# Layer 0's gathered context rows: 16 instead of 45 of the second tile's picks are left to the beginning of layer 1

## The chip, the cores and the metric

The kernel runs on one core of a Trainium2 chip. The metric is the device time of one execution in microseconds (us); lower is better. PE is TensorE, DVE is VectorE, ACT is ScalarE, POOL is GpSimd, SP is the SyncE queue that issues most transfers.

## What is computed

Two layers of a hybrid mixer (RWKV-7, latent attention and Hyena side by side) work on 512 latent and 256 context tokens of width 1024. Each layer ends in a PEER feed-forward: every token picks 16 of 16,384 one-neuron experts in each of 8 heads, so 128 picks a token:

```python
act = jax.nn.gelu(jnp.einsum('thkd,td->thk', exp_u[e_idx], xc), approximate=False)
return jnp.einsum('thk,thkd->td', gate * act, exp_v[e_idx])
```

In layer 0 the feed-forward serves both streams; the context's result is needed as input of layer 1's context projection.

## The kernel before

The program is written for a framework that orders the instructions of each engine by priority (mostly program order) and gives each engine one queue in that order. An engine works its queue off strictly in order.

**Layer 0's feed-forward (`ffn`, L1509)** treats its six 128-token tiles in two ways. Four latent tiles go through a *dense pass*: a loop over 128 blocks `n` of 128 experts. For a block the kernel loads `uT` (scores, 512 KB) and the second half of `uv` (values, 512 KB), rounds each into a high and a low part (`wh` by ACT at L657, `wl` by DVE at L658), multiplies the tokens by `uT` (`product`), applies gelu (`g`, ACT, L1544), multiplies by the gate weights `W` (DVE, L1608; a 1 MB load `W<-Wd` every four blocks), splits the result (`ch` ACT, `cl` DVE, L1612) and multiplies by the values. Three tiles accumulate in PSUM, the fourth (`acc3`) is added up by DVE at L1635, two blocks at a time, out of the PSUM tag `mm`, which has two buffers and serves the scores too. The scores of 44 of the 128 blocks are made earlier (`early`) and only loaded (`gl<-gd`). The loads go into a ring of three buffers `w`: SP issues a load when DVE has finished the `wl` of three loads before.

**Gathered rows (`Picks`, L181).** The two context tiles go another way: for pick `k` of a tile, POOL issues one indirect transfer (L203) that brings, for each of 128 tokens, the 8 KB row of the chosen expert (1 MB in all). DVE multiplies its first half by the tokens and sums (L219), ACT does gelu and the gate (L236, L237), DVE adds the second half into `acc` (L241). There are 256 such picks: 128 of the first context tile, then 128 of the second. Five row buffers are used in the dense pass, four behind it.

**Who does how many.** `NP = picks.n - REST` (L1590) is the number that the dense pass fetches: it spreads them over its blocks in proportion to `done`, so many scored blocks of `total = 212`:

```python
base, NP = len(picks.rows), picks.n - (0 if li else REST)
...
picks.fetch(min(base + 3 + (NP - base) * done // total, NP))
```

The other `REST` picks of the second tile are fetched by `gather` from `context_out`, one of four program tracks that `weave` merges at layer 1's beginning by a virtual clock; each pick advances that clock by `GC = 2.8`:

```python
while len(p.rows) < p.n - rest:
    p.fetch(len(p.rows) + 1)
    yield cost
p.use(p.n - rest)
```

After the last pick `ffn_out` transposes `acc` (L1503), scales it and stores the context. Beside this track run: `project` (the latents' projection with 21 weight tiles of 512 KB, 8 fp32 matrix products each, `mm<-h,wh`; each tile advances the clock by 6), then the context's projection, which waits for the context and for the filters; `hyena_filters` (two halves with products `hy<-...`, DVE writes `st`, which is stored as `coef<-st`); and later the RWKV scan.

Of the kernel before, what the change touches and what calls it, by code (L numbers as in the profile page):

```python
# [151 lines left out]
PB, RL, ML = 0.7, 0.42, 1.0  # L152
HL, HL1 = 1.0, 1.0
GP = 0.0
REST, GC = 45, 2.8
GS = 2.0 ** 14
SK = 44
WB, GB, UD = (2, 2), (1, 1), 1
# [1646 lines left out]
```

## Time and profile before

| what | value |
|---|---|
| median of 3 runs | 5381.51 us (5369.8 to 5392.99) |
| the profiled execution's own time | 5380.15 us |
| its span, first to last instruction | 5378.2 us |
| PE busy | 4894.6 us (91%) |
| DVE busy | 3836.6 us (71%) |
| mean granted TensorE clock | 0.935 |
| transfers | 1028.17 MB, mean 191 GB/s |

The profile is of one execution; 1.95 us of its time lie outside its span. Layer 0's dense pass runs from about 1834 to 3019 us, the beginning of layer 1 that this change touches from there to about 3320 us. A busy share over the whole span says little about either; the rows below are cut to these stretches.

### The profile page before, as it was taken

The page shows a single profiled execution, that of the slowest core. Times are in us where ns is not written, and L with a number is a line of the kernel's source. Part 1 is how long each engine was busy: PE and PEld are TensorE (multiplying, and loading weights), DVE is VectorE, ACT ScalarE, POOL GpSimd, SP SyncE. Part 2 cuts the span into 40 slices and gives each one's busy share as a digit, 9 for nine tenths or more (in the row PEclk, how much of TensorE's full clock was granted, in tenths as well). Part 3 has the DMA queues.
Part 4 walks back from the last instruction along what each step waited for, and adds up shares of the span by engine and source line. Part 5 has one row for each costly group of instructions (what it writes and reads, how often), then busy time and mean ns, then how long its engine had stood idle before and what let it go on. Part 6 is the DMA issues. An engine that isn't in the chain of part 4 may idle for free. (4 is left out here: it accounts for less than half of the span.)

```text
span 5378.2 us, 75892 instructions
## 1 busy us (share of the span) xinstructions
PE 4894.6 (91%) x28685; PEld 3719.0 (69%) x28685; DVE 3836.6 (71%) x8311; ACT 1918.1 (36%) x3416; POOL 1118.1 (21%) x869
## 2 busy tenths in 40 slices
PE   7987898889989999999999789888889999999998
PEld 4765676546746788877877435656647578888887
DVE  6456766755898688878888874766646986777776
ACT  5322222343256433333333222222223354444442
POOL 2222211222200122222222241211122101111110
PEclk8987898889999999999999889877889999999999
DMA  6300121342266888888888873200022678888885
GB/s 199 111 26 30 53 87 56 98 142 91 95 180 206 272 315 323 318 317 311 319 315 315 300 282 125 73 1 1 1 75 81 199 223 302 320 323 311 327 316 207
DMA packets 392491, 1028.17 MB, mean 191 GB/s; under 512 B 31443, under 2 KB 198644, under 8 KB 336572
## 3 DMA queue, kind: packets, MB, share of 16 engines
q1 hardware_dynamic: 336828, 620.64, 34.4%
q0 software_dynamic: 55296, 402.68, 19.7%
q8 instruction: 225, 3.69, 0.3%
q14 instruction: 142, 1.16, 0.1%
HBM read 920.19 MB, written 103.02 MB: 190 GB/s over the span
## 5 line engine op out<-in xcount | busy, mean ns | idle before, releaser
L203 POOL DMA_INDIRECT row<-in_uv,idx x384 | 535.6, 1395 | 2033.7 <-DVE acc L241 1853.8
L657 ACT ACTIVATE wh<-w 128x1024 fp32r<-128x1024 f32 x535 | 566.6, 1060 | 1037.0 <-PE mm L272 471.1
L272 PE MATMUL mm<-hlo,wh 128*128 128x512 f32 (+2 forms) x2400 | 863.9, 364 | 16.4 <-DVE acc L1635 6.8
L272 PE MATMUL mm<-hhi,wh 128*128 128x512 f32 (+2 forms) x2400 | 859.9, 362 | 0.0
L658 DVE TENSOR_TENSOR wl<-w,wh 128x1024 fp32r<-128x1024 f32 x466 | 568.4, 1223 | 295.5 <-ACT wh L657 272.7
L272 PE MATMUL mm<-hhi,wl 128*128 128x512 f32 (+2 forms) x2400 | 523.6, 359 | 0.0
L272 PEld LDWEIGHTS mm<-hlo,wh 128*128 128x128 f32 x2400 | 456.0, 190 | 84.0 <-issue 9.9
L241 DVE SCALAR_TENSOR_TENSOR acc<-row,act,acc 128x1024 f32<-128x1024 f32 x381 | 491.8, 1291 | 30.4 <-ACT act L237 29.9
L272 PEld LDWEIGHTS mm<-hhi,wh 128*128 128x128 f32 x2400 | 456.6, 190 | 60.1 <-issue 4.5
L219 DVE SCALAR_TENSOR_TENSOR row<-row,xk 128x1024 f32<-128x1024 f32 x384 | 473.2, 1233 | 18.3 <-DMA row<-in_uv,idx 17.3
L272 PEld LDWEIGHTS mm<-hhi,wl 128*128 128x128 f32 x2400 | 421.9, 188 | 51.7 <-issue 1.9
L272 PE MATMUL mm<-row,wh 128*128 128x384 f32 (+1 forms) x736 | 296.6, 546 | 6.7 <-ACT g L1544 4.4
L236 ACT ACTIVATE act<-act 128x1 f32<-128x1 f32 x384 | 75.9, 198 | 527.8 <-DVE row L219 527.6
L658 POOL TENSOR_TENSOR wl<-w,wh 128x1024 fp32r<-128x1024 f32 x69 | 165.8, 2408 | 424.5 <-PE mm L272 226.0
L1781 ACT ACTIVATE stage<-ch 128x512 f32<-128x512 f32 x224 | 220.4, 1110 | 64.3 <-PE ch L272 63.5
L272 PEld LDWEIGHTS mm<-row,wh 128*128 128x128 f32 x736 | 134.0, 193 | 113.8 <-issue 67.2
L272 PE MATMUL rw<-wh,cl 128*128 128x512 f32 x512 | 202.0, 394 | 7.7 <-DMA w<-in_uT 3.2
L272 PE MATMUL mm<-h,wh 128*128 128x512 f32 (+1 forms) x480 | 193.7, 550 | 13.4 <-DMA w<-in_hw 10.6
L272 PE MATMUL rw<-wl,ch 128*128 128x512 f32 x512 | 201.3, 393 | 0.0
L272 PE MATMUL rw<-wh,ch 128*128 128x512 f32 x512 | 200.4, 391 | 0.0
L272 PE MATMUL ch<-wh,cl 128*128 128x512 f32 x512 | 200.4, 391 | 0.0
L272 PE MATMUL ch<-wh,ch 128*128 128x512 f32 x512 | 200.0, 391 | 0.0
(541 smaller groups left out, 10296.2 us busy)
## 6 DMA issues: line engine op xcount, KB each, us to landing
w<-in_uv SPq DMA_DIRECT2D x256, 512.0 KB
w<-in_uT SPq DMA_DIRECT2D x210, 512.0 KB
Wd<-stage SPq DMA_DIRECT2D x28, 2048.0 KB
w<-in_mod_w SPq DMA_DIRECT2D x192, 256.0 KB
W<-Wd SPq DMA_DIRECT2D x32, 1024.0 KB
W<-Wd SPq DMA_DIRECT2D x32, 768.0 KB
wh<-in_uT SPq DMA_DIRECT2D x46, 512.0 KB
w<-in_wq SPq DMA_DIRECT2D x32, 512.0 KB
```

The lines of the kernel that those rows point to most:

```text
L203: self.nc.gpsimd.indirect_dma_start(out=row, out_offset=None, in_=self.k.io[f"uv{self.li}"], in_offset=bass.IndirectOffsetOnAxis(ap=self.t ...
L219: nc.vector.scalar_tensor_tensor(row[:, 0:1024], row[:, 0:1024], 1.0, self.x, op0=OP.mult, op1=OP.mult, accum_out=act)
L236: nc.scalar.activation(act, act, AF.Gelu)
L241: nc.vector.scalar_tensor_tensor(self.acc, row[:, 1024:], act, self.acc, op0=OP.mult, op1=OP.add)
L272: self.nc.tensor.matmul(out, lhsT, rhs, start=start, stop=stop, skip_group_check=True)
L657: self.nc.scalar.activation(wh[:, s], w, AF.Copy)
L658: eng.tensor_tensor(wl[:, s], w, wh[:, s].bitcast(F32), op=OP.subtract)
L1781: nc.scalar.activation(stage[:, :, u:u + 4].rearrange("p a t -> p t a"), p, AF.Copy, scale=1 / GS)
```

## The change

One number. `GC` and the code stay as they are.

```diff
-REST, GC = 45, 2.8
+REST, GC = 16, 2.8
```

So `NP` becomes 240 instead of 211, and `gather` in `context_out` fetches 16 rows instead of 45. The framework's order moves accordingly. Three places are shown.

POOL's queue where layer 1 begins; the two MEMSETs prepare layer 1's context keys and values, L203 is a gathered row of the second context tile, L1296 and L1297 belong to the Hyena filters. Before:

```order
L203 DMA row<-in_uv,idx_11414 128x2048 x122
L203 DMA row<-in_uv,idx_11415 128x2048 x92
L460 MEMSET kTc 1x1536
L462 MEMSET Vc 128x6x64
L203 DMA row<-in_uv,idx_11415 128x2048 x16
L1296 TENSOR_TENSOR hs<-hh 128x256
L1297 TENSOR_TENSOR hd<-hh 128x256
L203 DMA row<-in_uv,idx_11415 128x2048
```

The same place in the changed kernel:

```order
L203 DMA row<-in_uv,idx_11414 128x2048 x121
L203 DMA row<-in_uv,idx_11415 128x2048 x120
L460 MEMSET kTc 1x1536
L462 MEMSET Vc 128x6x64
L203 DMA row<-in_uv,idx_11415 128x2048 x8
L1296 TENSOR_TENSOR hs<-hh 128x256
L1297 TENSOR_TENSOR hd<-hh 128x256
L1296 TENSOR_TENSOR hs<-hh 128x256
```

Behind the MEMSETs stood 36 gathers (16 in one piece, 20 strewn between filter work), and now stand 8; ahead of them there are 28 more.

DVE's queue in the dense pass, from the `cl` of its tenth block on (`row,act<-row,xk` and `acc<-row` are the two halves of a pick, `wl` the low part of a load, `acc_16907` the fourth tile's sum). Before:

```order
L1612 TENSOR_TENSOR cl<-g,ch 128x512
L219 SCALAR_TENSOR_TENSOR row,act<-row,xk 128x1024
L241 SCALAR_TENSOR_TENSOR acc<-row,act,acc 128x1024
L658 TENSOR_TENSOR wl<-w,wh 128x1024
L1635 TENSOR_TENSOR acc_16907<-acc_16907,mm 128x512 x2
L658 TENSOR_TENSOR wl<-w,wh 128x1024
L1612 TENSOR_TENSOR cl<-gl,ch 128x512
```

In the changed kernel:

```order
L1612 TENSOR_TENSOR cl<-g,ch 128x512
L219 SCALAR_TENSOR_TENSOR row,act<-row,xk 128x1024
L241 SCALAR_TENSOR_TENSOR acc<-row,act,acc 128x1024
L658 TENSOR_TENSOR wl<-w,wh 128x1024
L1635 TENSOR_TENSOR acc_16907<-acc_16907,mm 128x512
L219 SCALAR_TENSOR_TENSOR row,act<-row,xk 128x1024
L241 SCALAR_TENSOR_TENSOR acc<-row,act,acc 128x1024
L1635 TENSOR_TENSOR acc_16907<-acc_16907,mm 128x512
L658 TENSOR_TENSOR wl<-w,wh 128x1024
L1612 TENSOR_TENSOR cl<-gl,ch 128x512
```

A second pick has moved in between the two sums, ahead of the next `wl`. Over the whole dense pass DVE's queue holds 241 picks instead of 214.

DVE's queue at layer 1's beginning, where the first filter's coefficients `st` are written (L685 and L686 are the convolution of a projected tile). Before:

```order
L1322 TENSOR_TENSOR st<-hy,rhy 128x2x128
L219 SCALAR_TENSOR_TENSOR row,act<-row,xk 128x1024
L241 SCALAR_TENSOR_TENSOR acc<-row,act,acc 128x1024
L219 SCALAR_TENSOR_TENSOR row,act<-row,xk 128x1024
L241 SCALAR_TENSOR_TENSOR acc<-row,act,acc 128x1024
L1322 TENSOR_TENSOR st<-hy,rhy 128x2x128
L241 SCALAR_TENSOR_TENSOR acc<-row,act,acc 128x1024
L219 SCALAR_TENSOR_TENSOR row,act<-row,xk 128x1024
L685 SCALAR_TENSOR_TENSOR zl<-mm,conv,zl 128x511
```

In the changed kernel:

```order
L1322 TENSOR_TENSOR st<-hy,rhy 128x2x128
L685 SCALAR_TENSOR_TENSOR zl<-mm,conv,zl 128x511
L686 SCALAR_TENSOR_TENSOR zl<-mm,conv,zl 128x511
L1322 TENSOR_TENSOR st<-hy,rhy 128x2x128
L804 TENSOR_SCALAR zl<-zl 128x512
L1332 TENSOR_TENSOR st<-hy,rhy 1x2x128
```

No pick is left between the filters' instructions; up to the filters' first sine (about 3088 us in the trace of before) DVE's queue there reads the same in both kernels.

## Rows read from the trace of the kernel before

**Rows 1.** Windows: length, busy us of PE, PEld, DVE, ACT, POOL; clock, DMA.

```profile
1850.00:3000.00 1150.00, 1123.90 (x4884) 920.44 (x4883) 933.27 (x1178) 408.65 (x812) 304.23 (x203) 0.99 0.85 317
3088.00:3224.50 136.50, 108.48 (x262) 51.81 (x261) 109.95 (x155) 31.16 (x81) 57.71 (x41) 0.90 0.78 284
3224.50:3319.00 94.50, 90.54 (x278) 47.14 (x277) 31.30 (x80) 14.25 (x26) 18.00 (x23) 1.00 0.42 137
4600.00:5200.00 600.00, 600.00 (x2972) 537.74 (x2971) 459.65 (x585) 246.65 (x466) 99.82 (x87) 1.00 0.87 321
```

**Rows 2.** Waits, 1850 to 3000 us: us in total, times, longest.

```profile
ACT wh L657 <- DMA w<-in_uT: 180.5, 57, 7.9
DVE acc L1635 <- PE mm L272: 63.1, 38, 3.4
...
PE mm L272 <- ACT g L1544: 19.3, 10, 2.5
...
PE mm L272 <- DVE acc L1635: 6.8, 5, 5.3
```

**Rows 3.** SP timeline: start, us, instruction.

```profile
2406.24 0.33 SPq L656 DMA_DIRECT2D w<-in_uT  x1
```

**Rows 4.** ACT timeline, same place.

```profile
2415.39 1.06 ACT L657 ACTIVATE wh<-w 128x1024 fp32r<-128x1024 f32 x1 [4.55 <-DMA w<-in_uT]
2416.35 0.58 ACT L1544 ACTIVATE g<-mm 128x512 f32<-128x512 f32 x1
```

**Rows 5.** PE timeline, same place.

```profile
2409.19 0.39 PE L272 MATMUL rw<-wh,cl 128*128 128x512 f32 x1
...
2414.43 0.39 PE L272 MATMUL hy<-wl,ch 128*128 128x512 f32 x1
2416.98 0.50 PE L272 MATMUL mm<-wh,cl 128*128 128x512 f32 x1 [2.17 <-ACT g L1544]
```

**Rows 6.** PE's waits, 3088 to 3224.5 us.

```profile
PE hy L272 <- DVE st L1326: 7.3, 1, 7.3
PE hy L272 <- DVE acc L241: 6.7, 1, 6.7
...
PE hy L272 <- ACT h L1245: 2.5, 1, 2.5
...
PE mm L272 <- issue: 2.0, 1, 2.0
```

**Rows 7.** DVE groups, 3088 to 3224.5 us: count, busy us, mean ns, idle.

```profile
L241 DVE SCALAR_TENSOR_TENSOR acc<-row,act,acc 128x1024 f32<-128x1024 f32 x30 | 41.4, 1379 | 0.9 <-ACT act L237 0.6
L219 DVE SCALAR_TENSOR_TENSOR row<-row,xk 128x1024 f32<-128x1024 f32 x29 | 39.7, 1368 | 2.9 <-DMA row<-in_uv,idx 2.7
```

**Rows 8.** DVE timeline in the dense pass, one pick and the next.

```profile
2425.83 1.23 DVE L219 SCALAR_TENSOR_TENSOR row<-row,xk 128x1024 f32<-128x1024 f32 x1
...
2428.17 1.23 DVE L219 SCALAR_TENSOR_TENSOR row<-row,xk 128x1024 f32<-128x1024 f32 x1
```

**Rows 9.** DMA queues, 1850 to 3000 us: packets, MB, share of 16 engines.

```profile
DMA packets 69124, 364.15 MB, mean 317 GB/s; under 512 B 7685, under 2 KB 7685, under 8 KB 39183
q0 software_dynamic: 29318, 213.45, 48.4%
```

**Rows 10.** ACT timeline: the last projected latent tiles leave PSUM.

```profile
3298.49 0.60 ACT L267 ACTIVATE zl<-mm 128x512 f32<-128x512 f32 x1 [5.51 <-PE mm L272]
3305.36 0.60 ACT L267 ACTIVATE zl<-mm 128x512 f32<-128x512 f32 x1 [5.61 <-PE mm L272]
```

**Rows 11.** PE by group, 3088 to 3224.5 us.

```profile
L272 PE MATMUL mm<-h,wh 128*128 128x512 f32 x176 | 84.3, 629 | 2.0 <-issue 2.0
L272 PE MATMUL hy<-hs,flt 128*128 128x256 f32 x32 | 9.7, 456 | 7.7 <-DVE acc L241 6.7 <-DMA flt<-in_fltl 0.9
```

**Rows 12.** PE timeline: a filter group without a gather in flight.

```profile
3263.27 1.91 PE L272 MATMUL hy<-hs,flt 128*128 128x256 f32 x8
3265.02 3.60 PE L272 MATMUL mm<-h,wh 128*128 128x512 f32 x8
```

## The prediction

> **What bounds the kernel now.** I read the windows first, since the share over the span mixes stages with different limits [rows 1]. In layer 0's dense pass TensorE is busy 1123.90 of 1150 us at a granted clock of 0.99; it sets the pace. But two others run close behind: VectorE is busy 933.27 us (81%), so 217 us idle, and the 16 DMA engines are 85% busy at 317 GB/s. Layer 1's dense pass shows the same load on the DMA engines (0.87, 321 GB/s) with TensorE busy 600 of 600 us, and VectorE there at 77%.
>
> The layer 1 beginning looks different. From 3088 to 3224.5 us, as long as gathered rows arrive, TensorE is busy 108.48 of 136.5 us at clock 0.90, VectorE 109.95, the DMA engines 78%. In the 94.5 us behind it, with the picks done, the same kind of work (projection and second filter) leaves TensorE idle only 4.0 us, at clock 1.00, with VectorE at 33%. So in the first stretch TensorE waits, and in the second it sets the pace. Its waits there [rows 6] name VectorE in the two long cases: 7.3 us for `st` and 6.7 us for `acc`, both filter products held up by VectorE's queue.
>
> Then I read who waits in the dense pass [rows 2]. TensorE loses 19.3 us in 10 waits for ScalarE's `g`, and 6.8 us for VectorE's sum. One of the ten shows how: SP issues the `uT` load at 2406.24 [rows 3]; ScalarE stands idle 4.55 us and casts it at 2415.39, 9.15 us later, and only behind that cast comes `g`, at 2416.35 [rows 4]. Meanwhile TensorE has worked through its other products from 2409.19 to 2414.8, some 5.6 us, and then waits 2.17 us for the `mm` buffer that `g` has to empty [rows 5]. So a late load costs nothing until it is about 5.6 us late. 57 of the `uT` loads found ScalarE waiting, 180.5 us in all [rows 2]; ten went past the cover.
>
> **What is gained in layer 1.** 29 picks lie between 3088 and 3224.5 us [rows 7]; up to 3088 VectorE's order is the same in both kernels, and behind it one pick is left. So 28 picks leave this stretch, 28 x (1.379 + 1.368) = 77 us of VectorE's time and 28 transfers of 1 MB. TensorE's own work in the stretch: 176 records of the projection [rows 11], 16 to a tile, are 11 tiles; undisturbed, a tile takes 3305.36 - 3298.49 = 6.87 us [rows 10], so 75.6 us. 8 filter groups (32 records for `hs` [rows 11], as many for `hd`, 8 to a group) at 3265.02 - 3263.27 = 1.75 us [rows 12] are 14.0 us. For the smaller products I put 7 us, an estimate: eight of about 0.9 us, half a filter group each. Together 97 us, against 136.5 us: 39.5 us are lost, 28.0 idle and 11.5 to slow clock. Not all comes back. The second filter still idles 4.0 us without any gather [rows 1], and the first one has two waits that are not due to picks, 2.5 us for the sine and 2.0 us with no releaser [rows 6]: 8.5 us idle, with slow clock in the ratio seen (11.5/28.0) 12 us. **Gain 27.5 us.** Bounds: 36 if only the 4.0 us remain (39.5 - 4.0); 20 if only the two waits that name VectorE's `st` and `acc` go, 14.0 us with their slow clock (14.0 x 1.41). What is late next is TensorE itself: the projection and filters run into the context's projection with the same order as before.
>
> **What is paid in the dense pass.** 27 more picks are in VectorE's queue there. From one `L219` to the next it takes 2.34 us [rows 8], so 27 x 2.34 = 63 us more VectorE work in 1150 us: 81% becomes 87%. The cover is VectorE's idle 217 us; 63.1 of it is waiting for TensorE itself [rows 2], and in the order a moved pick stands between just those two sums. 203 gathers moved 213.45 MB [rows 9], 1.05 MB each; 27 more are 28.4 MB on 364.15, 7.8%: the DMA share becomes 0.92.
>
> Both make `uT` loads later. The load's 9.15 us should grow with the bytes that share the engines, 8% or 0.7 us. A scored block holds two picks ahead of the next `wl`, now 2.26 on average: 0.26 x 2.34 = 0.6 us. So each load is late by 1.3 us more. The ten waits grow by 1.3 each, 13 us. Of the other 47 late loads, if their lateness is spread evenly over the cover of 5.6 us, 1.3/5.6 or 11 go past it, by 0.65 on average: 7 us. **Loss 20 us.** Below, it is bounded by nothing (all picks fall into idle time); above, by VectorE's full 63 us. I take the value near the lower third because TensorE still has the larger share and its wait gives VectorE time back.
>
> On the shared transfers: the row shows a load that needed 9.15 us at a DMA share of 0.85 [rows 1, 3, 4]. The Trainium skill ("DMA: Bandwidth & Descriptors", "Issuing engines are not separate DMA queues") says that transfers started by different engines run on the same 16 DMA engines and interleave, so gathers from GpSimd would delay SP's loads; that speaks against the change. By that rule the load part of the loss stands and the sum is about 5373; if gathers had a path of their own, the loss would be 20 x 0.6/1.3 = 9 us and the sum 5362. No row of before separates the two.
>
> Ahead of the dense pass the order holds one pick more: 2.3 us at most, taken as nothing. Behind layer 1's beginning the order is the same.
>
> **Sum.** 5380.15 (the profiled execution's own time, 0.03% under the median of 5381.51) - 27.5 + 20 = 5373 us, 0.14% less: no change that can be told, since about 0.5% (27 us) is what a measurement of this kernel can tell from none. Its own range, with gain 20 to 36 and loss 8 to 45, is 5352 to 5405.
>
> **Rivals.** *The picks are free in the dense pass.* Then loss 0 to 3 us, gain 27.5 to 36: 5344 to 5353, faster. For it: VectorE's 217 us idle, and layer 1's pass without a TensorE wait at nearly the same DMA share. Against: that pass has VectorE at 77%, this one at 81% already waits ten times.
>
> *VectorE takes the pace (the other sign).* If VectorE's queue with 87% and its waits for `W`, casts and gelu has no slack left, each moved pick costs its full 2.34 us where it stands: loss 63, 5380 + 63 - 27.5 = 5416, slower. It decides from a loss of 54 us, 2.0 us a pick. For it: the load ring turns only when VectorE has done `wl`, so its lateness feeds back. Against: 217 us idle against 63 added.
>
> *Transfers take the pace.* Here the gathers fill the engines so that loads come 3 us later, not 0.7: 10 x 3 + 47 x (3/5.6) x 1.5 = 68 us, 5421, slower. For it: the share goes to 0.92, the idle part from 0.15 to 0.08. Against: layer 1 at 0.87 shows no TensorE wait at all. The Trainium skill's section named above is the rule behind this one.
>
> *The picks leave, but layer 1's beginning stays as long*, since the filters' chain (products, VectorE, `coef` stores) holds TensorE as before: gain 5 to 10, loss 20, about 5393, no change. Against it: the second filter in the 94.5 us.
>
> **Chances.** My forecast 0.45; free picks 0.27; VectorE's pace 0.15; transfers' pace 0.07; no gain in layer 1 0.06. So faster by over 0.5% 0.27, within 0.5% 0.51, slower 0.22. The range of 5343 to 5417 holds the first case, most of the second and the edge of the third.
>
> **What would show it.** In the profile after: TensorE's idle time from 3088 us on (shifted by the dense pass's change) to the first context product should fall from 28 to about 9 us, at clock near 0.97; the two waits of 7.3 and 6.7 us are gone. The dense pass should be about 20 us longer, its waits for `g` 19.3 -> 35 to 40 us, VectorE at 86 to 87%, DMA share 0.90 to 0.92. I am wrong if the pass grows by over 50 us (VectorE's idle in it then under 100 us), if its length stays within 3 us, or if filter products wait as long as before without picks.

## The result, and the profile after

The changed kernel takes 5410.72 us (median of 7 runs, 5400.15 to 5434.52) against 5381.51 us (7 runs, 5369.8 to 5394.18): ratio 1.0056, 95% interval 1.0038 to 1.0073. It is slower by 0.56%, where I forecast 5373 us and no change that can be told. The profiled execution took the median's 5410.72 us, 30.6 us more than that of before.

To see where they went, I cut both traces at points that every kernel here passes: the first `row` that DVE takes out of PSUM at L760 (1201.6 us before), the first transposition of `spread` (L1756, the gate weights for the dense pass), the first ACT eviction of `acc` (L1633, the dense pass begins), the first transposition of `gl` (L1710, it has ended), and the last `hy<-ident,us` of layer 1's first phase (L1364, 3472.1 us before). The numbers are differences of these starts, in us.

| stretch | before | after | change |
|---|---|---|---|
| start to L760 | 1201.6 | 1208.0 | +6.4 |
| to L1756: candidates, early picks | 310.9 | 320.3 | +9.4 |
| to L1633: `spread` | 337.6 | 336.1 | -1.5 |
| to L1710: dense pass | 1169.3 | 1205.0 | +35.7 |
| to the last L1364: layer 1's beginning | 452.7 | 430.0 | -22.7 |
| the rest | | | +3.3 |

The first row and the rest have the same instruction order in both kernels and in all runs below, where they take 1195.0 to 1211.0 and 1894.3 to 1916.8 us. So their 6.4 and 3.3 us cannot be put down to the change. The changed stretches give +9.4 + 35.7 - 22.7 = 22.4 us; the medians differ by 29.

**Layer 1's beginning.** From `h<-hy,hv` (L1273, the filters' first row of VectorE behind the pass) to the first `hy<-ident,us` (L1364) TensorE does the same work in both kernels. The windows, before first, then after (the columns are those of [rows 1]):

```profile
3089.00:3318.90 229.90, 198.38 (x536) 98.89 (x537) 140.25 (x234) 45.40 (x107) 75.38 (x64) 0.94 0.63 223
```

```profile
3138.20:3344.30 206.10, 194.45 (x537) 97.84 (x537) 71.67 (x150) 29.32 (x49) 29.01 (x38) 0.97 0.34 110
```

The stretch is 23.8 us shorter. TensorE's idle time falls from 31.5 to 11.7 us, its busy time by 3.9 us, while its granted clock rises from 0.94 to 0.97; VectorE's busy time falls from 140.25 to 71.67. TensorE's waits in that stretch of after (compare [rows 6]):

```profile
PE hy L272 <- POOL qs L1302: 6.4, 2, 3.3
PE hy L272 <- ACT h L1245: 1.7, 1, 1.7
PE mm L272 <- issue: 1.2, 1, 1.2
```

The 7.3 us for `st` and the 6.7 us for `acc` are gone. What is left is mostly GpSimd's `qs`, 6.4 us (3.8 before).

**The dense pass.** Two windows over the whole pass, before first, then after:

```profile
1850.10:3019.40 1169.30, 1143.20 (x4968) 936.38 (x4967) 952.52 (x1202) 414.39 (x829) 310.73 (x208) 0.99 0.85 316
```

```profile
1864.40:3069.40 1205.00, 1160.14 (x4969) 946.15 (x4969) 1015.99 (x1285) 429.38 (x883) 351.23 (x235) 0.98 0.88 330
```

The pass grows by 35.7 us in two nearly equal parts. TensorE's idle time goes from 26.1 to 44.9 us, 18.8 more. And its busy time goes from 1143.20 to 1160.14 for the same number of matmuls, 16.9 more: they run slower, at a granted clock of 0.98 instead of 0.99. VectorE still has 189 us idle. Its waits and TensorE's in that stretch of after (compare [rows 2]):

```profile
PE mm L272 <- ACT g L1544: 30.2, 14, 4.1
PE mm L272 <- DVE acc L1635: 14.7, 9, 3.2
...
DVE acc L241 <- ACT act L237: 54.1, 27, 3.8
...
DVE acc L1635 <- PE mm L272: 36.0, 25, 3.4
...
DVE row L219 <- DMA row<-in_uv,idx: 11.5, 4, 3.4
```

The entry that has grown most is the third: VectorE stands 54.1 us before sums (L241) whose gelu ScalarE has not done. Before it was 28.7 us:

```profile
DVE acc L241 <- ACT act L237: 28.7, 26, 3.4
```

What hardly grows is ScalarE's waiting for `uT` loads over the pass, before and after:

```profile
ACT wh L657 <- DMA w<-in_uT: 180.5, 57, 7.9
```

```profile
ACT wh L657 <- DMA w<-in_uT: 185.5, 56, 8.6
```

From issue to cast, the loads that ScalarE waited for took 8.00 us in the median before and 8.02 after.

**One such place, followed along.** Rows of the timelines of ScalarE, VectorE, SP and TensorE of after, around 2125 us (start, duration, instruction, idle time ahead of it):

```profile
2121.44 1.23 DVE L219 SCALAR_TENSOR_TENSOR row<-row,xk 128x1024 f32<-128x1024 f32 x1
...
2124.88 1.06 ACT L657 ACTIVATE wh<-w 128x1024 fp32r<-128x1024 f32 x1 [6.55 <-DMA w<-in_uT]
2125.84 0.18 ACT L236 ACTIVATE act<-act 128x1 f32<-128x1 f32 x1
...
2126.26 0.58 ACT L1544 ACTIVATE g<-mm 128x512 f32<-128x512 f32 x1
2126.39 1.28 DVE L241 SCALAR_TENSOR_TENSOR acc<-row,act,acc 128x1024 f32<-128x1024 f32 x1 [3.71 <-ACT act L237]
...
2127.59 0.69 DVE L1608 TENSOR_TENSOR g<-g,W 128x512 f32<-128x512 f32 x1
2128.20 1.22 DVE L658 TENSOR_TENSOR wl<-w,wh 128x1024 fp32r<-128x1024 f32 x1
...
2129.48 0.33 SPq L656 DMA_DIRECT2D w<-in_uT  x1
...
2138.54 1.06 ACT L657 ACTIVATE wh<-w 128x1024 fp32r<-128x1024 f32 x1 [4.46 <-DMA w<-in_uT]
2139.50 0.58 ACT L1544 ACTIVATE g<-mm 128x512 f32<-128x512 f32 x1
...
2140.13 0.80 PE L272 MATMUL mm<-wh,cl 128*128 128x512 f32 x1 [4.07 <-ACT g L1544]
2140.72 0.63 PE L272 MATMUL mm<-wh,ch 128*128 128x512 f32 x1
```

Read it from the top. A product (L219) is done at 2122.6. Its gelu needs 0.2 us, but in ScalarE's queue it stands behind the cast of a `uT` load that is not there yet; ScalarE waits 6.55 us for that. VectorE, with the sum next in its own queue, waits 3.71 us. The late cast also holds back the `g` at 2126.26, which stands behind it in ScalarE's queue and which VectorE's L1608 needs. That `g` is done at 2126.84, so without the sum L1608 could have begun some 0.7 us earlier than 2127.59: of the 3.71 us, only these are the sum's own. Behind L1608 comes the `wl` at 2128.20, and with it the buffer comes free for which SP issues the next `uT` load, at 2129.48. That load takes 9.06 us until its cast, no longer than the 9.15 us of [rows 3, 4]; it was issued late. The `g` behind its cast is late, and TensorE waits 4.07 us. So one late load makes a later one late, by way of what VectorE has between the two: a pick's sum and the product with `W`.

The load of [rows 3] in the kernel before came the same way. VectorE's timeline there:

```profile
2403.16 1.29 DVE L241 SCALAR_TENSOR_TENSOR acc<-row,act,acc 128x1024 f32<-128x1024 f32 x1 [3.38 <-ACT act L237]
2404.36 0.69 DVE L1608 TENSOR_TENSOR g<-g,W 128x512 f32<-128x512 f32 x1
2404.96 1.22 DVE L658 TENSOR_TENSOR wl<-w,wh 128x1024 fp32r<-128x1024 f32 x1
```

SP issues at 2406.24, when this `wl` is done.

The clock follows. Windows of after ahead of that wait and behind it:

```profile
2110.00:2136.00 26.00, 26.00 (x115) 21.14 (x113) 22.29 (x28) 7.50 (x18) 8.89 (x6) 1.00 0.90 330
2140.00:2148.00 8.00, 7.87 (x29) 6.38 (x30) 7.55 (x11) 3.87 (x7) 0.00 (x0) 0.81 0.79 290
```

TensorE was busy throughout at full clock (1.00, that is 2.4 GHz), stood still 4.07 us, and then the granted clock in the rows is 0.81 over the next 8 us: some of that time at 1.2 GHz, the rest at 2.4. Of TensorE's waits over 3 us there are eight in the pass after, one before.

**Ahead of the dense pass.** VectorE's timeline of after, in the second tile's candidates:

```profile
1495.06 1.23 DVE L219 SCALAR_TENSOR_TENSOR row<-row,xk 128x1024 f32<-128x1024 f32 x1 [6.53 <-DMA row<-in_uv,idx]
1496.21 0.08 DVE L219 DVE_READ_ACCUMULATOR row<-row,xk 128x1 f32 x1
...
1496.48 1.28 DVE L241 SCALAR_TENSOR_TENSOR acc<-row,act,acc 128x1024 f32<-128x1024 f32 x1
```

and GpSimd's (L203 is the gather):

```profile
1481.59 6.33 POOL L1457 TENSOR_TENSOR ci<-sf 128x128 f32<-128x128 f32 x7 [11.10 <-DVE c L1465]
1488.07 1.30 POOL L203 DMA_INDIRECT row<-in_uv,idx  x1
```

The one pick more stands in the middle of the chain that selects experts. VectorE waits 6.53 us for a row (the last gather issued before is that of 1488.07, behind 6.33 us of `ci`), and with product and sum that makes 6.53 + 1.23 + 1.28 = 9.0 us. The kernel before issues this gather too, but uses its row only much later.

### The profile page after: what moved, and what is told of

The parts are those of the page before. It is cut to its first block, busy times and chain, and to the rows that moved or that the text cites. A ratio compares the mean times of both kernels' runs of the same rounds, so it can differ in the third digit from the quotient of the medians.

```text
span 5409.0 us, 75860 instructions
## 1 busy us (share of the span) xinstructions
PE 4926.1 (91%) x28685; PEld 3739.1 (69%) x28685; DVE 3829.6 (71%) x8311; ACT 1919.8 (35%) x3413; POOL 1112.6 (21%) x869
## 5 line engine op out<-in xcount | busy, mean ns | idle before, releaser
L203 POOL DMA_INDIRECT row<-in_uv,idx x384 | 537.2, 1399 | 2021.6 <-DVE acc L241 1836.1
L272 PE MATMUL mm<-hlo,wh 128*128 128x512 f32 (+2 forms) x2400 | 868.9, 366 | 24.4 <-DVE acc L1635 14.7
L241 DVE SCALAR_TENSOR_TENSOR acc<-row,act,acc 128x1024 f32<-128x1024 f32 x381 | 488.9, 1283 | 55.4 <-ACT act L237 55.3
L219 DVE SCALAR_TENSOR_TENSOR row<-row,xk 128x1024 f32<-128x1024 f32 x384 | 469.0, 1221 | 33.8 <-DMA row<-in_uv,idx 32.0
L272 PEld LDWEIGHTS mm<-row,wh 128*128 128x128 f32 x736 | 134.8, 194 | 122.7 <-issue 68.7
```

The costliest lines, as they stand in the source:

```text
L203: self.nc.gpsimd.indirect_dma_start(out=row, out_offset=None, in_=self.k.io[f"uv{self.li}"], in_offset=bass.IndirectOffsetOnAxis(ap=self.t ...
L219: nc.vector.scalar_tensor_tensor(row[:, 0:1024], row[:, 0:1024], 1.0, self.x, op0=OP.mult, op1=OP.mult, accum_out=act)
L241: nc.vector.scalar_tensor_tensor(self.acc, row[:, 1024:], act, self.acc, op0=OP.mult, op1=OP.add)
L272: self.nc.tensor.matmul(out, lhsT, rhs, start=start, stop=stop, skip_group_check=True)
```

## The experiments

All times are medians. All ratios are to the kernel before, timed beside them (its medians: 5385.31 us for e1 to e4, 5385.17 for e5 to e8, 5381.20 for e9 to e11, 5382.88 for e12 and e13). The three stretches are those of the table above, of one profiled execution each. Where the order is the same, two kernels show the spread: before and e1 differ by 1.9 us in the pass and by 0.1 up to L1756, after and e2 by 6.0 in the pass. The profiled executions of e8 and e10 lie 20 and 19 us under their medians, in part outside these stretches. Code cuts are marked with `...`.

| run | picks in the pass + left | to L1756 | dense pass | layer 1's beginning | us | ratio (95%) |
|---|---|---|---|---|---|---|
| before | 211 + 45 | 310.9 | 1169.3 | 452.7 | 5381.51 | 1 |
| after | 240 + 16 | 320.3 | 1205.0 | 430.0 | 5410.72 | 1.0056 (1.0038 to 1.0073) |
| e1 | 211 + 16 | 311.0 | 1171.2 | 428.9 | 5365.2 | 0.996 (0.9939 to 0.998) |
| e2 | 240 + 45 | 319.6 | 1211.0 | 455.1 | 5442.45 | 1.0093 (1.0072 to 1.0114) |
| e3 no transfer | 240 + 16 | 318.3 | 1181.4 | 429.5 | 5372.72 | 0.9977 (0.996 to 0.9994) |
| e4 no sum | 240 + 16 | 317.6 | 1177.8 | 429.7 | 5377.84 | 0.998 (0.9964 to 0.9997) |
| e5 two at most | 240 + 16 | 310.2 | 1184.6 | 430.6 | 5374.32 | 0.9981 (0.9965 to 0.9997) |
| e6 uneven | 211 + 45 | 309.7 | 1184.3 | 464.4 | 5410.09 | 1.0035 (1.002 to 1.0051) |
| e7 30 left | 226 + 30 | 318.6 | 1194.9 | 436.0 | 5411.4 | 1.0039 (1.0018 to 1.0061) |
| e8 later sums | 240 + 16 | 319.6 | 1183.8 | 422.3 | 5386.1 | 0.9999 (0.9983 to 1.0014) |
| e9 both mends | 240 + 16 | 317.9 | 1176.2 | 420.8 | 5373.63 | 0.9989 (0.9968 to 1.001) |
| e10 before, later sums | 211 + 45 | 317.2 | 1139.1 | 452.4 | 5355.33 | 0.9961 (0.994 to 0.9982) |
| e11 both mends, 4 left | 252 + 4 | 319.5 | 1186.4 | 410.7 | 5356.9 | 0.9955 (0.9937 to 0.9974) |
| e12 as e9, no transfer | 240 + 16 | 318.1 | 1167.8 | 418.8 | 5360.75 | 0.9963 (0.9943 to 0.9984) |
| e13 as e9, no sum | 240 + 16 | 318.9 | 1198.8 | 418.1 | 5393.87 | 1.0023 (1.0009 to 1.0038) |

### e1 and e2: the two halves of the change by themselves

e1, on the changed kernel:

```diff
-            picks.pool(gp, 4)
+            picks.pool(gp, 4); picks.n -= 0 if li else 29
```

> 29 of the 256 picks are left out altogether: the dense pass does the same picks as in the kernel before, in the same order, and layer 1's beginning has 16 as in the changed kernel. This is the gain in layer 1 alone. My prediction's step (27.5 us, bounds 20 to 36): about 5353, ratio 0.995. What the two profiles show (layer 1's beginning 22 us shorter): 5358 to 5360. Rival, that the gain there depends on what the dense pass left in the queues (gathers already under way, clock): under 10 us, over 5370. In all cases the dense pass takes 1169 us as before, and the stretches ahead of it too; where those differ by some us, that is the spread of one execution.

Layer 1's beginning is 23.8 us shorter, the whole 20 us.

e2, with `REST = 45` and 29 picks more:

```diff
-            picks.pool(gp, 4)
+            picks.pool(gp, 4); picks.n += 0 if li else 29
...
-            yield from self.gather(128 * (1 - j), GC)
+            yield from self.gather(157 * (1 - j), GC)
...
```

> 29 picks are added: the dense pass has 240 as in the changed kernel, layer 1's beginning still 45 (29 rows of the second tile are gathered and summed twice). This is the cost ahead of layer 1 alone. If the parts add up: 5381 plus 36 (dense pass) plus 8 to 15 (ahead of it) = 5425 to 5432, ratio 1.008 to 1.009. My prediction's step (20 us): 5401, 1.004. Rival, that part of what the dense pass loses is given back later (its late end meets a layer 1 that waits less): under 5400.

It costs 57 us in the medians, 41.7 of the profile's in the pass and 8.7 ahead of it. The halves add up: 1.0093 and 0.996 make 1.0053, and the change measures 1.0056. So no part of the loss is seen to be given back later.

### e3 and e4: VectorE's work or the transfers

e3 lets 28 picks of the pass use the row of the pick before; e4 gathers 29 and leaves their product and sum out (`repeat` and `skip` pick every eighth or so, evenly):

```diff
         while len(self.rows) < min(n, self.n):
+            if self.repeat(): continue
...
```

```diff
         while self.used < min(n, len(self.rows)):
+            if self.skip(): continue
...
```

> The changed kernel, but 28 picks of the dense pass work on the row of the pick before them: VectorE and ScalarE do all 240 picks, the transfers of 28 of them are left out (so the output has these picks' terms wrong). Theory of the queue (VectorE's longer queue makes loads' casts and sums late): the dense pass stays 30 us or more longer than in the kernel before, about 1200, and the whole 5405 or more. Theory of the transfers (gathers delay the loads): the dense pass returns to about 1172 to 1180 and the whole to 5375 to 5385. Both in equal parts: about 1185 and 5393.

> The changed kernel, but 28 or 29 picks of the dense pass are gathered and not used: all 240 transfers, VectorE's and ScalarE's work for 211 only (these picks are missing in the output). Theory of the queue: the dense pass is back at 1170 to 1180 us, the whole at 5370 to 5385. Theory of the transfers: it stays at about 1200, the whole at 5400 or more. If each alone costs little and only both together much, this run and the one without transfers both come out near 5380 (an interaction).

Both come out at 5373 and 5378, the case that e4's text called an interaction. VectorE's work alone costs the pass 12.1 us, the transfers alone 8.5, both together 35.7. That speaks against a bound of VectorE or of the DMA engines by itself. (In e3 fewer rows also mean more free buffers, and in e4 the left-out picks break up groups, so it is not shown that the two meet in one place; the next runs look at the groups.)

### e5, e6, e7: three picks in a row

By the formula of L1662 the pass hands out 211 picks over 212 steps of `done`, under one a step; a block has one or two steps, and no block gets more than two picks (the first excepted). With 240 it is over one a step, and 20 blocks get three; with 226, 10 blocks. In VectorE's queue most of these threes are broken up by other work: three picks in a row stand there in 8 places of after and 4 of e7, three between one `wl` and the next in 16 and 8; before has none of either. e5 keeps 240 and hands out two at most (four behind the first block, as before):

```diff
-                picks.fetch(min(base + 3 + (NP - base) * done // total, NP))
+                picks.fetch(min(base + 3 + (NP - base) * done // total, NP, len(picks.rows) + (2 if n else 4)) if not li else ...)
```

> The changed kernel with at most two picks behind each block (four behind the first, as before): same 240 picks, same transfers, but none of the 20 places where three stand in a row; the ones over are made up behind the blocks that had one. Theory of the bursts (three picks are 7 us of VectorE in one piece, more than the cover): the dense pass falls from 1205 to 1172 to 1182 us, the stall ahead of it goes too, and the whole is about 5360 to 5370, ratio 0.997. Theory of the load (VectorE's and the DMA engines' total, each over the cover only together): the dense pass stays at 1195 or more and the whole at 5395 to 5405.

The pass falls from 1205.0 to 1184.6 us, the 9 us ahead of it go, the whole is 36 us faster than the changed kernel: the same picks and the same bytes, only laid out otherwise. The pass stops 3 us above what the theory of the bursts gave, so 15 us are left. VectorE's waits of sums for gelu are not what went; in the pass of e5 they are

```profile
DVE acc L241 <- ACT act L237: 52.5, 27, 4.0
```

e6 is the test from the other side, before's 211 picks with 20 threes, made up by ones:

```diff
-                picks.fetch(min(base + 3 + (NP - base) * done // total, NP))
+                picks.fetch(min(base + 3 + (NP - base) * done // total, NP) if li else len(picks.rows) + int(MARKS[n]))
...
```

> The kernel before (45 picks left to layer 1, 211 in the dense pass) with the picks laid out unevenly: the 20 blocks that have three in the changed kernel have three here, and 49 of its blocks with two have one. Theory of the bursts: the dense pass grows from 1169 to 1185 to 1205 us with no more work in it, the whole to 5395 to 5420. Theory of the load: it stays within 4 us of 1169, and the whole within 0.1% of the kernel before.

15.0 us more in the pass without any more work, the whole 25 us slower, not all of it by the pass. (25 blocks go from two picks to one, not the 49 of the text above.) That ends the theory that only totals count. But here the waits of sums for gelu are fewer than before's 28.7 us:

```profile
DVE acc L241 <- ACT act L237: 11.8, 7, 2.9
```

So the layout costs 15 us (e6), the 29 picks laid out evenly cost 15 (e5), both together 36. How a three does it, the runs do not show: it is not by sums that wait for gelu, and not on the spot. Of TensorE's 44.8 us of waits in the pass of after, 4 come within 20 us of the start of a stretch with three picks between two `wl`; nearly all of the others follow 25 to 39 or 65 to 75 us behind it. (Another 11.7 us are lost in layer 1's beginning, where VectorE's and TensorE's rows stand in another order and the context's transposition, L1503, comes later. I had not expected that, and did not follow it.)

> 30 picks left to layer 1, half way. Half the gain there is 11 us, and 10 blocks have three picks instead of 20. Theory of the bursts: half the loss too, 18 us in the dense pass, plus the stall of 9 us ahead of it: about 5385 to 5395. Theory of the load, where a loss appears only once lateness passes the cover (convex): under 8 us in the dense pass, the whole 5372 to 5382.

(`REST = 30`, nothing else.) This misses both theories: half the picks and half the threes cost 25.6 us in the pass and 7.7 ahead of it, more than half of what 29 cost, and the whole is 5411 us against the 5385 to 5395 of the bursts. With a gain of 16.7 it is as slow as the change. So the loss is not in proportion to the threes. One pick a step is 212 picks, and 45 left, with 211, lies just under that; whether the loss sets in there, no run between 211 and 226 shows.

### e8, e9, e10: sums that don't wait for gelu

A pick's sum follows two products behind its own instead of one:

```diff
-            self.finish()
-            self.last = (j, k, row, act)
+            self.finish(0 if self.li else 1)
+            self.last += [(j, k, row, act)]
...
-                self.use(held[-bufs] + 2)
+                self.use(held[-bufs] + (2 if self.li else 3))
...
```

The edit does a second thing: products come one pick earlier and lie more evenly. Of the stretches between two `wl`, 81 of before hold two products, 55 of e10; 16 of after hold three, 10 of e8.

> The changed kernel, but a pick's sum is put two products behind its own instead of one, so that ScalarE's gelu has one more product's time. Theory that VectorE's 54 us of waiting for gelu (29 before) make the loss: these waits fall to under 25 us, the dense pass to 1180 to 1190, the whole to 5385 to 5395. Rival: each row stays in its buffer one pick longer (five buffers), gathers start later, and VectorE waits for rows instead: the whole at 5410 or more.

VectorE's and TensorE's waits in the pass of e8:

```profile
PE mm L272 <- DVE acc L1635: 19.8, 13, 3.1
PE mm L272 <- ACT g L1544: 16.3, 6, 4.3
...
DVE row L219 <- DMA row<-in_uv,idx: 85.0, 44, 5.1
```

The waits of sums for `act`, 54.1 us, are gone altogether, the pass is 21.2 us shorter and the whole 25 us faster than the changed kernel. The rival's sign is there too: rows are held one pick longer, and VectorE waits 85.0 us for gathered rows instead of 11.5. It costs less than it saves. (Layer 1's beginning is 7.7 us shorter than after's too, which I did not follow.)

> Both mends on the changed kernel: at most two picks behind a block, and each sum two products behind its own. If they remove different parts (bursts; sums that wait for a gelu behind a late cast), the gains of 36 and 25 us add in part: 5345 to 5360, faster than the kernel before by 0.5% or a little more. If they remove the same lateness, about 5370 as with the cap alone.

The mends overlap: 5373.63, no better than the cap alone.

> The kernel before (45 left) with only the later sums. Theory of the feedback through gelu: VectorE waits for it only 29 us there, so little is gained: 5375 to 5385, and against this kernel the changed one with later sums (5386) is no slower. Rival, that later sums help any layout alike (25 us): 5355 to 5365, and then the 29 moved picks still cost what they did.

Here my theory missed and the rival held. Before gains 26 us by later sums, as much as the changed kernel does. The window of its pass, and TensorE's waits there:

```profile
1848.40:2987.50 1139.10, 1133.84 (x4969) 931.29 (x4967) 950.92 (x1199) 414.56 (x829) 296.13 (x208) 1.00 0.86 323
```

```profile
PE mm L272 <- DVE acc L1635: 3.6, 7, 1.7
...
DVE gl L1608 <- DMA W<-Wd: 80.9, 20, 6.9
...
DVE row L219 <- DMA row<-in_uv,idx: 11.7, 5, 4.3
```

TensorE idles 5 us in 1139, at clock 1.00, and does not wait for `g` once, with the DMA engines as busy as before (0.86 and 0.85). So the ten waits of [rows 2] came from the order of VectorE's and ScalarE's work, and not from transfers that were slow. Whether from sums that wait for gelu (28.7 us before, none here) or from products that lie unevenly, this run does not separate. And it does not explain the change: with later sums in both, the 29 moved picks still make the pass 44.7 us longer (1139.1 to 1183.8), more than the 35.7 without, and the whole slower by 0.38% of the ratios, some 20 us (31 between the two medians).

### e11, e12, e13: what is left

> Both mends with only 4 picks left to layer 1 (252 in the dense pass, two behind every block). If the dense pass, once even, takes more picks at little cost, 12 more give 9 us more in layer 1 for 5 to 8 us: within 5 us of the run with both mends. If VectorE's queue is then the bound (each pick 2.34 us): over 15 us slower than that.

5356.9, 17 us under e9, which neither case expected, though the two profiled executions have nearly the same span (5370.2 and 5368.4): twelve picks more in the pass cost it 10.2 us and give 10.1 in layer 1. Where the 17 us are is not shown. At 0.85 us a pick, under the 2.34 us of VectorE's work, VectorE is not the bound there.

e12 and e13 are e3's and e4's edits on e9:

> The run with both mends (two at most behind a block, later sums, 16 left), but 28 picks of the dense pass work on the row of the pick before them: all of VectorE's work, 28 transfers fewer (these picks' terms are wrong in the output). With later sums the pass took 1139 us with 211 picks and 1176 with 240, and VectorE's waits for gathered rows went from 12 to 96 us. If the rest of the cost comes from the gathers (rows that come late, buffers held longer): the dense pass near 1145 to 1155, the whole 5340 to 5350. If VectorE's work makes it: 1170 or more, the whole within 5 us of 5374.

> The same, but 29 picks of the dense pass are gathered and not used: all transfers, VectorE's work for 211 (these picks are missing in the output). If VectorE's work makes the rest of the cost: the dense pass 1140 to 1155 and the whole 5340 to 5350. If the gathers make it: 1170 or more and the whole within 5 us of 5374. Both fast means again that each alone is covered and only both together pass it.

Without 28 transfers the whole is 13 us faster and the pass 8.4 us shorter than e9's, short of what the theory of the gathers gave; VectorE's waits for rows fall as it said, e9 first, then e12:

```profile
PE mm L272 <- DVE acc L1635: 30.1, 17, 3.3
...
DVE row L219 <- DMA row<-in_uv,idx: 95.7, 43, 3.8
```

```profile
PE mm L272 <- DVE acc L1635: 16.6, 11, 3.3
...
DVE row L219 <- DMA row<-in_uv,idx: 10.7, 5, 3.7
```

Without 29 picks' VectorE work, e13 is 20 us slower than e9. Its edit has a side: GpSimd waits 134.8 us in all for a buffer whose unused row has still to land, and VectorE's waits for rows stay at 85.7 us. It shows that those waits do not come from VectorE's own work, but not what that work costs. Of the 37 us by which the pass of e9 is longer than that of e10, some 8 are the transfers'; the other 29 stay open. TensorE's waits in e12 name VectorE's sum out of `mm` (L1635), 16.6 us against 3.6 in e10, which points at the picks' work in VectorE's queue; but e13, without that work, has 21.5 us of them.

## Why the prediction was wrong

**Layer 1's gain: right.** 27.5 forecast, bounds 20 to 36; 22.7 in the profile, 23.8 in e1. The two waits went. Of the 27.5, 19.5 were idle time and 8 slow clock; the same work idled 19.9 us less and ran 3.9 us faster. So the idle part was right, and the clock gave back half. What I had not named is GpSimd's `qs`, 6.4 us. The rival that layer 1's beginning stays as long is out.

**"One pick more, 2.3 us at most, taken as nothing": failed.** 9.4 us. I priced VectorE's work on that pick and not its wait for the row, in a place where the selection of experts is behind it in the queue. The four kernels that have no third product of a pick there (before, e1, e5, e6) take 309.7 to 311.0 us up to L1756; the eleven that have one take 317.2 to 320.3. e10 is the test: four gathers there as in the kernel before, but one product more, and the wait is there:

```profile
1480.24 1.23 DVE L219 SCALAR_TENSOR_TENSOR row<-row,xk 128x1024 f32<-128x1024 f32 x1 [6.57 <-DMA row<-in_uv,idx]
```

**The dense pass: the step that failed most.** I said that both effects make each `uT` load late by 1.3 us, 0.7 from bytes and 0.6 from VectorE's mean of "2.26" picks, and came to 20 us of waits; the pass grew by 35.7. TensorE's idle time did grow by 18.8 us, but that the size is near is luck. The loads took no longer, 8.02 us from issue to cast against 8.00, and ScalarE waited 185.5 us for them instead of 180.5, where 1.3 us for each of the 57 would be 74. The waits for `g` grew less than forecast (30.2 us, not 35 to 40), and those for VectorE's sum out of `mm`, which had no term, from 6.8 to 14.7. VectorE came to 84% and the DMA engines to 0.88, both under the forecast, since the pass became longer. Three things were missing.

- *The layout instead of the mean.* The mean hides that 20 blocks have three picks. e5 and e6 show that the layout costs from both sides: 20 us less without the threes, 15 us more with them alone. How they cost it stays open, and e7 shows that it is not in proportion to their number.
- *The path of the lateness.* I took the ten waits for slow transfers plus a queue. e10 removes them with the bytes unchanged, and the rows show the path: from a late cast over a pick's gelu and the `g` behind it to VectorE, to `wl`, to the next load's issue. I had the rows of a wait's end [rows 3 to 5] and did not ask why SP issued that load when it did. This explains before's waits; what the 29 picks cost it does not, since with later sums they cost the pass 44.7 us.
- *The clock.* In layer 1 I had counted 11.5 us of slow clock beside 28.0 of waits; in the dense pass I counted none. It is 16.9 us beside 18.8. Not every wait brings it: in e4 TensorE idles 34.8 us, 8.7 more than before, and its matmuls take 1142.98 us at clock 1.00.

With 15.7 us missing in the pass, 9.4 ahead of it and 4.8 less gained, 30 of the 37.7 us between 5373 and the profiled 5410.72 are told; the rest lies in stretches whose order was not changed. The loss of pass and picks ahead of it together, 45.1 us, is at the end of the 8 to 45 that I had allowed, and those two numbers had not been worked out from rows.

**The rivals.** The time is near that of "VectorE takes the pace" (5416), but not for its reason: VectorE kept 189 us idle, not under 100, and e3, with all its work, gives most of the loss back. "Transfers take the pace" (5421) fails likewise by e4. "The picks are free" fails by e2. The truth lay between two of them, which I had costed one at a time: each alone costs 8 to 12 us, both 36. On the transfers the Trainium skill ("DMA: Bandwidth & Descriptors", "Issuing engines are not separate DMA queues") has gathers from GpSimd and loads from SP interleave on the same engines. e3 and e12 agree that 28 gathers fewer help (23.6 and 8.4 us in the pass); that single loads take longer, the traces do not show (8.02 against 8.00 us).

The two fastest versions that leave nothing out beat both kernels: before with later sums (5355.33), and 4 picks left with both mends (5356.9), 0.4% under the kernel before.

## What to carry to other kernels

When work is spread over a loop by a rate, look at how it is laid out over single rounds, not only at the mean: the same picks and bytes took 20 us less here (e5). Where two engines hand an item to and fro (product, gelu, sum), an in-order queue joins them to whatever else stands in either; putting the second half further behind gave 26 and 25 us (e10, e8; the same edit also spread the products more evenly). And when you price a wait of TensorE, ask for the matmuls behind it too.

## What the runs showed of the hardware that was not expected

The matmuls' slowing after waits cost the dense pass 16.9 us, nearly as much as the added waits themselves (18.8), while e4's waits cost nothing of the kind. Two stretches in unchanged order took between 1195.0 and 1211.0 us and between 1894.3 and 1916.8 us in 15 profiled executions, so a difference of 10 us between two single profiles says little where the order is the same.
